# Two-layer hybrid decoder trunk: the first x piece travels with the norm's scale columns, the first AV weights come in halves, and two k tiles multiply their high parts first

## The chip, the cores and the metric

The kernel runs on one core of one Trainium2 chip. The metric is device time in microseconds (us), median of several runs; lower is better. Before the change it is 254.97 us (median of 3 runs, 254.91 to 255.15).

The names of the engines in this text: PE is TensorE (matmuls; PEld is its weight load), DVE is VectorE, ACT is ScalarE, POOL is GpSimd, SP is SyncE. SP computes nothing here, it issues DMAs. ACT issues a few as well.

## The reference, cut to what matters

A sequence of 256 tokens with 1024 channels passes two layers. Each layer normalizes x, projects it with one combined matrix `w_in` (1024 x 3584) into ten pieces, runs three mixers on them (dilated attention A, a gated linear recurrence B, stick-breaking attention C), gates each and projects back with `w_out`.

```python
def hybrid_layer(x, ...):
    hn = rms_norm(x, norm_gain)
    proj = jnp.einsum('bsd,de->bse', hn, w_in)
    a_q, a_k, a_v, a_g, b_x, b_g, c_q, c_k, c_v, c_g = jnp.split(proj, _in_split_points(), axis=-1)
    y_a = dilated_attention(rope(a_q), rope(a_k), a_v) * jax.nn.silu(a_g)
    y_b = rg_lru_branch(b_x, ...) * jax.nn.silu(b_g)
    y_c = stick_breaking_attention(c_q, c_k, c_v) * jax.nn.silu(c_g)
    y = jnp.concatenate([y_a, y_b, y_c], axis=-1)
    return x + jnp.einsum('bse,ed->bsd', y, w_out)
```

`rms_norm` divides each token by the root of its mean square and multiplies each channel by `norm_gain`. The kernel may therefore multiply x by the channel gains first, run the projections of layer 0 on that, and divide by the root per token afterwards.

## The kernel before

**Precision.** Every large product is done in three fp32r matmuls. An operand is split into a high part (a rounded copy) and a low part (the operand less its high part), and high x high, low x high and high x low are added up in one PSUM bank. So each 128-row piece of x becomes `xh` and `xl`, each piece of weights `hi` and `lo` (tiles `whi`, `wlo`). ACT makes the high parts by a copy, DVE the low parts by a subtraction.

**The opening stage**, which the change rewrites, is the loop over `k` (lines 133 to 155). It computes two projections of layer 0 that need x as the stationary operand: AV (512 columns, two PSUM banks `s`, one for each half of the tokens) and CV (256 columns, two banks `pp`). There are NK = 8 pieces `k` of 128 channels. One DMA brings for a piece its transposed x (256 columns) and its AV and CV weights (512 + 256 columns) as one 128 x 1024 tile `st`; the pool has 5 such tiles, so pieces 5 to 7 are issued when an older tile has been read. ACT multiplies x by the gain column `g` while it copies it to `xh`, then copies the weights to `hi`; DVE makes `xl` and `lo`. PE then runs six pairs of matmuls for the piece: AV high, AV low x, AV low weights, CV high, CV low x, CV low weights, each for two halves of the tokens.

Piece 0 is special. It is fetched by three DMAs, x (128 KB) and the CV weights (128 KB) on SP's queue, the AV weights (256 KB) on ACT's. ACT's queue also brings `prm_t`, a table of small parameters with the gain columns at its end; every `xh` needs it. Its AV weights are rounded by DVE (line 144) rather than ACT:

```python
        act.activation(xh[:, k, :], st[:, 0:S], AF.Copy, scale=g)
        if k == 0:
            dve.tensor_copy(hi[:, 0:512], st[:, S:S + 512])
            act.activation(hi[:, 512:768], st[:, S + 512:1024], AF.Copy)
```

Ahead of the loop PE runs seven matmuls on zeros (line 131), and ACT loads its function table.

**After it** the remaining projections go chunk by chunk through `proj_b` (line 262; 48 matmuls of 256 columns a chunk, in two halves), in the order CQ, CK, AQ, AK, BX and so on. Each chunk's weights arrive as two DMAs on SP's queue (line 100), ACT rounds them in four copies (line 103) and DVE subtracts in four (line 104). Between the halves of CK, `rows_of_rstd` turns the token scales into a row (lines 293 to 299). Then `scaled` writes the stick-breaking query `qc` and key `kc` (line 311), and `sb_scores` (line 353) multiplies them on PE inside the AQ projection. `rp0` (line 500) is the rotary table times the token scales, used by `rotate` for AQ and AK. `sb_weights` (line 380) later multiplies `sh` and `sl`, the split softplus of the scores.

**Order.** PE's order is the order in which the code is written. ACT, DVE, POOL and SP are ordered by the framework's scheduler, so their streams may shift when the code changes. `log_sigmoid_lambda` (line 219) is a chain of tiny operations on POOL, DVE and ACT that reads `prm_t`; its result is needed by the recurrence much later.

Of the kernel before, what the change touches and what calls it, by code (L numbers as in the profile page):

```python
# [38 lines left out]
SM_P = 16  # L39
# [5 lines left out]


@with_exitstack
def trunk_kernel(ctx: ExitStack, tc: tile.TileContext, x, first, wpack, prm_d, gatew, gains, consts, rope, out):
    nc = tc.nc
    act, dve, pe, gps = nc.scalar, nc.vector, nc.tensor, nc.gpsimd  # L50

    cst = ctx.enter_context(tc.tile_pool(name="cst", bufs=1))
    wst = ctx.enter_context(tc.tile_pool(name="wst", bufs=WST))
    wsp = ctx.enter_context(tc.tile_pool(name="wsp", bufs=4))
    sb = ctx.enter_context(tc.tile_pool(name="sb", bufs=1))
# [36 lines left out]
    xh = sb.tile([P, NK, S], F32R, name="xh", tag="xh")  # L92
    xl = sb.tile([P, NK, S], F32R, name="xl", tag="xl")

    def load_chunk(l, c):
        hi = wsp.tile([P, 2048], F32R, name="whi", tag="whi")
        lo = wsp.tile([P, 2048], F32R, name="wlo", tag="wlo")
        for i in range(2):
            st = wst.tile([P, 1024], F32, name="st", tag="st")
            nc.sync.dma_start(out=st, in_=wpack[l, c][:, i * 1024:(i + 1) * 1024])  # L100
            for j in range(0, 1024, 512):
                ws, ss = slice(i * 1024 + j, i * 1024 + j + 512), slice(j, j + 512)
                act.activation(hi[:, ws], st[:, ss], AF.Copy)  # L103
                dve.tensor_sub(lo[:, ws], st[:, ss], hi[:, ws].bitcast(F32))  # L104
        return hi, lo
# [11 lines left out]

    cold = sb.tile([P, 512], BF16, name="cold", tag="th")
    dve.memset(cold, 0.0)
    prm_t = cst.tile([P, L * SM_P + NK], F32, name="prm_t")  # L120
    st0 = [wst.tile([P, 1024], F32, name="st", tag="st")]
    nc.sync.dma_start(out=st0[0][:, 0:S], in_=first[0][:, 0:S])
    act.dma_start(out=st0[0][:, S:S + 512], in_=first[0][:, S:S + 512])
    act.dma_start(out=prm_t, in_=prm_d)
    nc.sync.dma_start(out=st0[0][:, S + 512:1024], in_=first[0][:, S + 512:1024])
    table(LN_EXP)
    av_ps = [bank(at, "s") for _ in range(NT)]
    cv_bk = [bank(pp, "pp") for _ in range(NT)]
# [2 lines left out]
        pe.matmul(warm, cold[:, 0:P], cold, start=True, stop=True)  # L131
    pair = None
    for k in range(NK):
        st = st0[0] if k == 0 else wst.tile([P, 1024], F32, name="st", tag="st")
        if k > 0:
            nc.sync.dma_start(out=st, in_=first[k])
        g = prm_t[:, L * SM_P + k:L * SM_P + k + 1]
        if k % 2 == 0:
            pair = [wsp.tile([P, 2048], F32R, name=n, tag=n) for n in ("whi", "wlo")]
        o = k % 2 * 768  # L140
        hi, lo = [a[:, o:o + 768] for a in pair]
        act.activation(xh[:, k, :], st[:, 0:S], AF.Copy, scale=g)
        if k == 0:
            dve.tensor_copy(hi[:, 0:512], st[:, S:S + 512])
            act.activation(hi[:, 512:768], st[:, S + 512:1024], AF.Copy)
        else:
            act.activation(hi, st[:, S:1024], AF.Copy)
        dve.scalar_tensor_tensor(xl[:, k, :], st[:, 0:S], g, xh[:, k, :].bitcast(F32), ALU.mult, ALU.subtract)
        for c in ((0, 512), (512, 768)) if k == 0 else ((0, 768),):
            dve.tensor_sub(lo[:, c[0]:c[1]], st[:, S + c[0]:S + c[1]], hi[:, c[0]:c[1]].bitcast(F32))  # L150
        for ps, c in ((av_ps, slice(0, 512)), (cv_bk, slice(512, 768))):
            for i, (a, b) in enumerate(((xh, hi), (xl, hi), (xh, lo))):
                for t in range(NT):
                    pe.matmul(ps[t][:, 0:c.stop - c.start], a[:, k, t * P:(t + 1) * P], b[:, c],  # L154
                              start=k == 0 and i == 0, stop=k == NK - 1 and i == 2)
# [61 lines left out]
    nc8 = cst.tile([P, L * 2], F32, name="nc8")  # L217

    def log_sigmoid_lambda():
        lam = prm_t[:, 0:L * SM_P].rearrange("p (q j) -> p q j", q=2 * L)[:, :, 7:8].rearrange("p b j -> p (b j)")  # L220
# [28 lines left out]
    for l in range(L):  # L249
        prm = prm_t[:, l * SM_P:(l + 1) * SM_P].rearrange("p (b j) -> p b j", b=2)  # L250
        if l > 0:
            xh, xl = next_x
# [23 lines left out]
        if l > 0:  # L276
# [3 lines left out]
            av_ps, cv_ps = [], bank(pp, "pp")  # L280
# [7 lines left out]
            cv_bk = [cv_ps[:, t * 256:(t + 1) * 256] for t in range(NT)]  # L288
# [19 lines left out]
        def scaled(dst, ps, sc=1.0):  # L308
            if l == 0:
                a, b = rows(ps)  # L310
                dve.scalar_tensor_tensor(dst, a, sc, b, ALU.mult, ALU.mult)  # L311
            else:
                act.activation(dst, v2(ps), AF.Copy, scale=sc)
# [5 lines left out]
        gw = gw_t.rearrange("p (g b c) -> p g b c", g=2, b=2)  # L319
# [30 lines left out]
        kc = sb.tile([P, 2, S], F32, name="kc", tag="k1")  # L350
# [91 lines left out]
        it = sb.tile([P, 2, S], F32, name="it", tag="it")  # L442
# [53 lines left out]
        ck_ps = proj_b(CH_CK, rows_of_rstd if l == 0 else None)  # L496
        if l == 0:
            scaled(qc, cq_ps, 0.125)
            for i in range(2):
                dve.tensor_mul(rp0[:, i, :], rp[:, i, :], rb)  # L500
        scaled(kc, ck_ps)
        rotate(proj_b(CH_AQ[0], sb_scores), qT, 0, "q0")
        rotate(proj_b(CH_AK[0], lambda: sb_weights(0)), kT, 0, "k0")
        sb_weights(1)
# [128 lines left out]
    return wp  # L633


def _pack_small(norm_gain, conv_w, conv_b, gate_a_w, gate_a_b, gate_x_w, gate_x_b, lru_lambda):
    pr = np.zeros((P, L * SM_P + NK), np.float32)
    pr[:, L * SM_P:] = norm_gain[0].reshape(NK, P).T
    gw = np.zeros((P, L, SM_W), np.float32)
    for l in range(L):  # L640
        for b in range(2):
            r = slice(b * P, b * P + P)
            o = l * SM_P + 8 * b
            pr[:, o:o + 4] = conv_w[l][:, r].T
            pr[:, o + 4] = conv_b[l][r]
            pr[:, o + 5] = gate_a_b[l].reshape(-1)[r]
            pr[:, o + 6] = gate_x_b[l].reshape(-1)[r]
            pr[:, o + 7] = lru_lambda[l][r]
            for g, w in enumerate((gate_a_w, gate_x_w)):
                c = (g * 2 + b) * P  # L650
                for j in range(2):
                    gw[j * HD:(j + 1) * HD, l, c + j * HD:c + (j + 1) * HD] = w[l, 2 * b + j]
    return pr, gw


def _arrays(x, norm_gain, w_in, conv_w, conv_b, gate_a_w, gate_a_b, gate_x_w, gate_x_b,
            lru_lambda, w_out, final_gain):
# [32 lines left out]
```

## Time and profile before

| | |
|---|---|
| median of 3 runs | 254.97 us |
| the profiled execution's own time | 255.37 us |
| its span, first to last instruction | 253.6 us |
| PE busy | 245.1 us (97%) |
| DVE busy | 190.3 us (75%) |
| ACT busy | 164.2 us (65%) |
| POOL busy | 12.9 us (5%) |
| chain of work that ended last | PE 95%, DMA 1%, ACT 1% |
| bytes moved | 43.44 MB |

The profile is one execution. A row of the timeline has the start of a group of instructions and its length in us, the engine, the line, the operation, its output and input tiles, the shapes, how many it merges, and in brackets how long the engine sat idle before it and what ended that. An engine name with a q behind it (SPq, ACTq) is the engine's queue issuing a DMA; the length is then that of the issue, not of the transfer. Matmuls overlap, so the distance between the starts of two groups tells what a group costs. All times in this document are us from the first instruction of the span unless they are lengths.

### The profile page before, as it was taken

What the parts mean: (1) busy time and instruction counts of PE and PEld (TensorE: products, weight loads), DVE (VectorE), ACT (ScalarE), POOL (GpSimd) and SP (SyncE); (2) the same over time, 40 slices, a digit from 0 to 9 for tenths busy, and PEclk for the clock granted to TensorE, in tenths of its full rate; (3) what the DMA queues carried; (4) which work ended last, traced back from release to release, by engine and by line L of the source; (5) the groups of instructions that cost most, each with busy time, mean ns of one, the idle gap of its engine ahead of it and who ended that gap; (6) DMA issues with size and microseconds to landing.
All of it is one profiled execution on the core that took longest, in us unless ns stands there. A gap on an engine that the chain in (4) does not pass through costs nothing.

```text
span 253.6 us, 4715 instructions
## 1 busy us (share of the span) xinstructions
PE 245.1 (97%) x1771; PEld 223.7 (88%) x1771; DVE 190.3 (75%) x424; ACT 164.2 (65%) x355; POOL 12.9 (5%) x35
## 2 busy tenths in 40 slices
PE   6999999999999999999999999999999999999990
PEld 2889999998999989878889999999899998987870
DVE  4684498999999669988692754399999846984243
ACT  3767958953675875994762865593495596794143
POOL 1186000000000000000010000000000000000000
PEclk9999999999999999999999999999999999999999
DMA  6989988844337840158457486531734732000022
GB/s 195 363 270 386 349 297 307 283 190 145 105 121 230 269 159 14 59 188 257 162 173 240 138 291 237 168 123 45 226 109 156 233 109 84 3 0 0 3 83 83
DMA packets 12982, 43.44 MB, mean 171 GB/s; under 512 B 1568, under 2 KB 1952, under 8 KB 12960
## 3 DMA queue, kind: packets, MB, share of 16 engines
q1 hardware_dynamic: 12672, 42.87, 49.6%
q8 instruction: 14, 0.23, 0.3%
q10 hardware_dynamic: 288, 0.28, 0.3%
q14 instruction: 8, 0.07, 0.1%
HBM read 42.09 MB, written 1.05 MB: 170 GB/s over the span
## 4 chain that ended last, share of the span: by engine, by line
PE 95%; DMA 1%; ACT 1%; DVE 0%; issue 0%; SPq 0%; ACTq 0%
PE pp L195 65%; PE s L195 9%; PE s L154 5%; PE y L345 3%; PE pp L154 2%; PE s L413 2%; PE s L435 2%; PE s L386 1%; PE pp L461 1%; DMA st<-first 1%; PE s L359 1%; PE s L211 1%; PE s L366 0%; PE s L384 0%; PE s L362 0%; ACT scr L177 0%
## 5 line engine op out<-in xcount | busy, mean ns | idle before, releaser
L104 DVE TENSOR_TENSOR wlo<-st,whi 128x512 fp32r<-128x512 f32 x132 | 84.9, 686 | 22.4 <-ACT whi L103 21.3
L103 ACT ACTIVATE whi<-st 128x512 fp32r<-128x512 f32 x132 | 74.5, 623 | 28.6 <-PE pp L195 10.4
L195 PE MATMUL pp<-xh,whi 128*128 128x256 f32 x352 | 50.3, 285 | 0.0
L195 PE MATMUL pp<-xl,whi 128*128 128x256 f32 x352 | 49.4, 283 | 0.0
L195 PE MATMUL pp<-xh,wlo 128*128 128x256 f32 x352 | 49.4, 283 | 0.0
L195 PEld LDWEIGHTS pp<-xh,whi 128*128 128x128 f32 x352 | 45.8, 191 | 1.4 <-issue 1.3
L195 PEld LDWEIGHTS pp<-xh,wlo 128*128 128x128 f32 x352 | 45.4, 192 | 0.0
L195 PEld LDWEIGHTS pp<-xl,whi 128*128 128x128 f32 x352 | 45.4, 192 | 0.0
L82 ACT ACTIVATE pr<-scr,mn 128x128 f32<-128x128 f32 (+1 forms) x32 | 14.1, 441 | 10.3 <-DVE mn L421 10.3
L177 ACT ACTIVATE scr<-xres 128x512 f32<-128x512 f32 x12 | 7.5, 626 | 12.5 <-DVE xres L569 12.4
L195 PE MATMUL pp<-whi,yh 128*128 128x512 f32 x48 | 14.1, 394 | 0.0
L195 PE MATMUL pp<-whi,yl 128*128 128x512 f32 x48 | 13.8, 390 | 0.0
L195 PE MATMUL pp<-wlo,yh 128*128 128x512 f32 x48 | 13.8, 390 | 0.0
L333 ACT ACTIVATE yh<-scr 128x512 fp32r<-128x512 f32 x8 | 5.0, 631 | 13.1 <-DVE scr L332 13.1
L179 POOL TENSOR_SCALAR ss<-sq 128x1 f32<-128x1 f32 x6 | 1.8, 306 | 221.0 <-ACT scr L177 220.9
L76 ACT ACT_TABLE_LOAD x9 | 11.5, 1283 | 1.8 <-PEq L683 1.6
L82 ACT ACTIVATE scr<-scr 128x384 f32<-128x384 f32 (+1 forms) x20 | 10.8, 542 | 1.2 <-DVE scr L311 0.9
L195 PEld LDWEIGHTS pp<-wlo,yh 128*128 128x128 f32 x48 | 9.0, 188 | 1.9
L195 PEld LDWEIGHTS pp<-whi,yl 128*128 128x128 f32 x48 | 9.0, 188 | 1.9
L421 DVE CUSTOM_DVE_ANT_0 scr<-s,con 128x128 f32<-128x128 f32 (+1 forms) x32 | 10.2, 347 | 0.0
L195 PEld LDWEIGHTS pp<-whi,yh 128*128 128x128 f32 x48 | 8.7, 188 | 1.6
L569 DVE TENSOR_TENSOR xres<-pp,xres 128x512 f32<-128x512 f32 x6 | 4.1, 690 | 6.7 <-PE pp L195 6.6
(158 smaller groups left out, 360.0 us busy)
## 6 DMA issues: line engine op xcount, KB each, us to landing
st<-w_pack SPq DMA_DIRECT2D x66, 512.0 KB, 4.8
st<-first SPq DMA_DIRECT2D x7, 512.0 KB, 6.9
xres<-x_in SPq DMA_DIRECT2D x2, 512.0 KB, 8.3
out<-scr SPq DMA_DIRECT2D x4, 256.0 KB, 2.2
gw_t<-gate_w SPq DMA_DIRECT2D x2, 256.0 KB, 6.7
gn<-gains SPq DMA_DIRECT2D x1, 512.0 KB, 6.5
gf<-gains SPq DMA_DIRECT2D x1, 512.0 KB, 5.6
st<-first ACTq DMA_DIRECT2D x1, 256.0 KB, 3.2
```

What stands on the lines that cost most here:

```text
L76: load = act.preload_act_table_set(name)
L82: i = dep(act.activation(*a, **k), loaded["load"])
L103: act.activation(hi[:, ws], st[:, ss], AF.Copy)
L104: dve.tensor_sub(lo[:, ws], st[:, ss], hi[:, ws].bitcast(F32))
L154: pe.matmul(ps[t][:, 0:c.stop - c.start], a[:, k, t * P:(t + 1) * P], b[:, c], start=k == 0 and i == 0, stop=k == NK - 1 and i == 2)
L177: act.activation(scr(512), xres[:, t, i * 512:(i + 1) * 512], AF.Square, accum_out=sq[:, i:i + 1])
L195: pe.matmul(ps, a(k), b(k), start=first and i == 0, stop=last and i == len(seq) - 1)
L333: act.activation(yh[:, k0:k0 + n, :], dst, AF.Copy)
L345: pe.matmul(y[hr, p * 128 + o:p * 128 + 256], vt[:, s0, hs], wts[i][:, ws], start=s0 == 0, stop=s0 == 1)
L413: pe.matmul(sps[h][:, cs], qT[h0][hr, hb, t * P:(t + 1) * P], kT[h0][hr, hb, 0:(t + 1) * P], start=True, stop=True)
L421: dve.tensor_tensor_reduce(xs[:, cs], sps[h][:, cs], nmask[:, cs], -0.125, 3e38, ALU.add, ALU.min, mn[:, t:t + 1])
L435: pe.transpose(tp[:, i * P:(i + 1) * P], prob[h0 + h][:, j * P:(j + 1) * P], ident)
```

## The change

It does four things.

1. The gain columns leave `prm_t` and are put behind the x piece of `k` = 0 in an array of their own, `first_x` (128 x 264). One DMA at the head of SP's queue brings both into a tile `x0`. All eight gain columns are then read from `x0`. `prm_t`, now without them, is fetched on SP's queue behind the eight pieces of the loop.
2. The 512 AV weight columns of piece 0 come as two DMAs of 256 columns, one on ACT's queue and one on SP's; the 256 CV columns move to ACT's queue. DVE rounds the two halves apart, and PE multiplies them apart for `k` = 0 (256 columns instead of 512, twice as many matmuls of half the size).
3. For `k` = 0 and 1 PE runs all high x high products (AV and CV) first, then all with low x, then all with low weights. For `k` = 1 too, DVE rounds the AV weights and ACT only the CV weights.
4. `kc` is written ahead of the two products for `rp0`.

```diff
-    prm_t = cst.tile([P, L * SM_P + NK], F32, name="prm_t")
-    st0 = [wst.tile([P, 1024], F32, name="st", tag="st")]
-    nc.sync.dma_start(out=st0[0][:, 0:S], in_=first[0][:, 0:S])
-    act.dma_start(out=st0[0][:, S:S + 512], in_=first[0][:, S:S + 512])
-    act.dma_start(out=prm_t, in_=prm_d)
-    nc.sync.dma_start(out=st0[0][:, S + 512:1024], in_=first[0][:, S + 512:1024])
+    x0 = sb.tile([P, S + NK], F32, name="x0", tag="it")
+    st0 = wst.tile([P, 1024], F32, name="st", tag="st")
+    nc.sync.dma_start(out=x0, in_=first_x)
+    act.dma_start(out=st0[:, S:S + 256], in_=first[0][:, S:S + 256])
+    nc.sync.dma_start(out=st0[:, S + 256:S + 512], in_=first[0][:, S + 256:S + 512])
+    act.dma_start(out=st0[:, S + 512:1024], in_=first[0][:, S + 512:1024])
...
-        g = prm_t[:, L * SM_P + k:L * SM_P + k + 1]
+        x_in = x0 if k == 0 else st
+        g = x0[:, S + k:S + k + 1]
...
-        act.activation(xh[:, k, :], st[:, 0:S], AF.Copy, scale=g)
-        if k == 0:
-            dve.tensor_copy(hi[:, 0:512], st[:, S:S + 512])
-            act.activation(hi[:, 512:768], st[:, S + 512:1024], AF.Copy)
+        w = st[:, S:1024]
+        act.activation(xh[:, k, :], x_in[:, 0:S], AF.Copy, scale=g)
+        for c0, c1 in {0: ((0, 256), (256, 512)), 1: ((0, 512),)}.get(k, ()):
+            dve.tensor_copy(hi[:, c0:c1], w[:, c0:c1])
+        if k < 2:
+            act.activation(hi[:, 512:768], w[:, 512:768], AF.Copy)
         else:
-            act.activation(hi, st[:, S:1024], AF.Copy)
+            act.activation(hi, w, AF.Copy)
...
+        parts = ((av_ps, 0, 0, 256), (av_ps, 0, 256, 512)) if k == 0 else ((av_ps, 0, 0, 512),)
+        parts += ((cv_bk, 512, 512, 768),)
+        terms = tuple(enumerate(((xh, hi), (xl, hi), (xh, lo))))
+        seq = [(i, p) for i in terms for p in parts] if k < 2 else [(i, p) for p in parts for i in terms]
+        for (i, (a, b)), (ps, base, c0, c1) in seq:
+            for t in range(NT):
+                pe.matmul(ps[t][:, c0 - base:c1 - base], a[:, k, t * P:(t + 1) * P], b[:, c0:c1],
...
+    prm_t = cst.tile([P, L * SM_P], F32, name="prm_t")
+    nc.sync.dma_start(out=prm_t, in_=prm_d)
     ready[pending.pop(0)] = load_chunk(0, CH_CQ)
...
             scaled(qc, cq_ps, 0.125)
+        scaled(kc, ck_ps)
+        if l == 0:
             for i in range(2):
                 dve.tensor_mul(rp0[:, i, :], rp[:, i, :], rb)
-        scaled(kc, ck_ps)
```

**PE, pieces 0 and 1.** In these rows `s` are the AV banks, `pp` the CV banks, and the two tiles behind the arrow are the two operands. Before:

```order
L154 MATMUL s<-whi,xh 128x512 x2
L154 MATMUL s<-whi,xl 128x512 x2
L154 MATMUL s<-wlo,xh 128x512 x2
L154 MATMUL pp<-whi,xh 128x256 x2
L154 MATMUL pp<-whi,xl 128x256 x2
L154 MATMUL pp<-wlo,xh 128x256 x2
L154 MATMUL s<-whi,xh 128x512 x2
```

With the change, the same engine at the same place:

```order
L160 MATMUL s<-whi,xh 128x256 x4
L160 MATMUL pp<-whi,xh 128x256 x2
L160 MATMUL s<-whi,xl 128x256 x4
L160 MATMUL pp<-whi,xl 128x256 x2
L160 MATMUL s<-wlo,xh 128x256 x4
L160 MATMUL pp<-wlo,xh 128x256 x2
L160 MATMUL s<-whi,xh 128x512 x2
L160 MATMUL pp<-whi,xh 128x256 x2
L160 MATMUL s<-whi,xl 128x512 x2
L160 MATMUL pp<-whi,xl 128x256 x2
```

The CV products with high parts have moved ahead of the AV products with low parts; from piece 2 on the order is as it was.

**ACT, its first instructions.** `st<-first` are weights of piece 0, `x_85` is the new tile `x0`. Before:

```order
L123 DMA st<-first 128x512
L124 DMA prm_t<-prm 128x40
L76 ACT_TABLE_LOAD
L145 ACTIVATE whi<-st 128x256
L142 ACTIVATE xh<-st,prm_t 128x256 x2
L147 ACTIVATE whi<-st 128x768
```

With the change:

```order
L123 DMA st<-first 128x256
L125 DMA st<-first 128x256
L76 ACT_TABLE_LOAD
L144 ACTIVATE xh<-x_85 128x256
L148 ACTIVATE whi<-st 128x256
L144 ACTIVATE xh<-st,x_85 128x256
L148 ACTIVATE whi<-st 128x256
L144 ACTIVATE xh<-st,x_85 128x256
L150 ACTIVATE whi<-st 128x768
```

The copy of the x piece now stands ahead of the CV weights, waits for `x0` alone, and the weight copy of piece 1 is a third as wide.

**DVE, around the stick-breaking scores.** Here `whi`, `wlo` are chunks of the later projections, `kc` the key, `rp_285` and `rp_296` the scaled rotary table, `sh` and `sl` the split softplus of the first head. Before:

```order
L311 SCALAR_TENSOR_TENSOR qc<-pp,rb 128x512
L104 TENSOR_TENSOR wlo<-st,whi 128x512 x4
L500 TENSOR_TENSOR rp_285<-rp,rb 128x256 x2
L311 SCALAR_TENSOR_TENSOR kc<-pp,rb 128x512
L104 TENSOR_TENSOR wlo<-st,whi 128x512 x8
L374 SCALAR_TENSOR_TENSOR scr<-s,scr 128x384
L377 CAST sh<-scr 128x384
L104 TENSOR_TENSOR wlo<-st,whi 128x512
L378 TENSOR_TENSOR sl<-scr,sh 128x384
```

With the change:

```order
L320 SCALAR_TENSOR_TENSOR qc<-pp,rb 128x512
L104 TENSOR_TENSOR wlo<-st,whi 128x512 x4
L320 SCALAR_TENSOR_TENSOR kc<-pp,rb 128x512
L511 TENSOR_TENSOR rp_296<-rp,rb 128x256 x2
L104 TENSOR_TENSOR wlo<-st,whi 128x512 x7
L383 SCALAR_TENSOR_TENSOR scr<-s,scr 128x384
L104 TENSOR_TENSOR wlo<-st,whi 128x512
L386 CAST sh<-scr 128x384
L104 TENSOR_TENSOR wlo<-st,whi 128x512
L387 TENSOR_TENSOR sl<-scr,sh 128x384
```

`kc` stands two instructions earlier. The scheduler has also moved one weight subtraction of the eight behind the softplus.

More of the change, by code (lines that the diff above doesn't have):

```diff
@@ L47, in trunk_kernel @@
 @with_exitstack
-def trunk_kernel(ctx: ExitStack, tc: tile.TileContext, x, first, wpack, prm_d, gatew, gains, consts, rope, out):
+def trunk_kernel(ctx: ExitStack, tc: tile.TileContext, x, first_x, first, wpack, prm_d, gatew, gains, consts, rope, out):
     nc = tc.nc
@@ L133, in trunk_kernel @@
     for k in range(NK):
-        st = st0[0] if k == 0 else wst.tile([P, 1024], F32, name="st", tag="st")
+        st = st0 if k == 0 else wst.tile([P, 1024], F32, name="st", tag="st")
         if k > 0:
             nc.sync.dma_start(out=st, in_=first[k])
-        g = prm_t[:, L * SM_P + k:L * SM_P + k + 1]
+        x_in = x0 if k == 0 else st
+        g = x0[:, S + k:S + k + 1]
         if k % 2 == 0:
@@ L141, in trunk_kernel @@
         hi, lo = [a[:, o:o + 768] for a in pair]
-        act.activation(xh[:, k, :], st[:, 0:S], AF.Copy, scale=g)
-        if k == 0:
-            dve.tensor_copy(hi[:, 0:512], st[:, S:S + 512])
-            act.activation(hi[:, 512:768], st[:, S + 512:1024], AF.Copy)
-        else:
[L147 to L155, printed above, removed]
+        w = st[:, S:1024]
+        act.activation(xh[:, k, :], x_in[:, 0:S], AF.Copy, scale=g)
+        for c0, c1 in {0: ((0, 256), (256, 512)), 1: ((0, 512),)}.get(k, ()):
+            dve.tensor_copy(hi[:, c0:c1], w[:, c0:c1])
@@ new lines, in trunk_kernel @@
+        if k < 2:
+            act.activation(hi[:, 512:768], w[:, 512:768], AF.Copy)
+        else:
+            act.activation(hi, w, AF.Copy)
+        dve.scalar_tensor_tensor(xl[:, k, :], x_in[:, 0:S], g, xh[:, k, :].bitcast(F32), ALU.mult, ALU.subtract)
+        for c0, c1 in ((0, 512), (512, 768)) if k < 2 else ((0, 768),):
+            dve.tensor_sub(lo[:, c0:c1], w[:, c0:c1], hi[:, c0:c1].bitcast(F32))
+        parts = ((av_ps, 0, 0, 256), (av_ps, 0, 256, 512)) if k == 0 else ((av_ps, 0, 0, 512),)
@@ new lines, in trunk_kernel @@
+        parts += ((cv_bk, 512, 512, 768),)
[4 more added lines that the diff above has]
+                pe.matmul(ps[t][:, c0 - base:c1 - base], a[:, k, t * P:(t + 1) * P], b[:, c0:c1],
+                          start=k == 0 and i == 0 and c0 == base, stop=k == NK - 1 and i == 2,
+                          skip_group_check=True)
@@ L219, in log_sigmoid_lambda @@
     def log_sigmoid_lambda():
-        lam = prm_t[:, 0:L * SM_P].rearrange("p (q j) -> p q j", q=2 * L)[:, :, 7:8].rearrange("p b j -> p (b j)")
+        lam = prm_t.rearrange("p (q j) -> p q j", q=2 * L)[:, :, 7:8].rearrange("p b j -> p (b j)")
         def tn(name):
@@ L633, in _pack_weights, with _pack_small @@
     return wp
-def _pack_small(norm_gain, conv_w, conv_b, gate_a_w, gate_a_b, gate_x_w, gate_x_b, lru_lambda):
-    pr = np.zeros((P, L * SM_P + NK), np.float32)
-    pr[:, L * SM_P:] = norm_gain[0].reshape(NK, P).T
+def _pack_small(conv_w, conv_b, gate_a_w, gate_a_b, gate_x_w, gate_x_b, lru_lambda):
+    pr = np.zeros((P, L * SM_P), np.float32)
     gw = np.zeros((P, L, SM_W), np.float32)
@@ L661, in _arrays @@
     x2 = x.reshape(S, D)
-    pr, gw = _pack_small(norm_gain, conv_w, conv_b, gate_a_w, gate_a_b, gate_x_w, gate_x_b, lru_lambda)
+    pr, gw = _pack_small(conv_w, conv_b, gate_a_w, gate_a_b, gate_x_w, gate_x_b, lru_lambda)
     return {
         "x_in": np.ascontiguousarray(x2),
+        "first_x": np.concatenate([x2.T[0:P], norm_gain[0].reshape(NK, P).T], 1),
         "first": np.concatenate([x2.T.reshape(NK, P, S), w_in[0].reshape(NK, P, 3584)[:, :, 1024:1536],
```

## The prediction

> **What bounds the kernel now.** I read the page first, then PE's waits, then the timeline of the opening.
>
> ```profile
> span 253.6 us, 4715 instructions
> ...
> PE 245.1 (97%) x1771; PEld 223.7 (88%) x1771; DVE 190.3 (75%) x424; ACT 164.2 (65%) x355; POOL 12.9 (5%) x35
> ```
>
> PE works nearly all the span. The view of its waits lists one besides that for its very first operand:
>
> ```profile
> PE s L154 <- ACT xh L142: 0.9, 1, 0.9
> ```
>
> From its first real matmul on, PE never waits. The change leaves PE's products the same, so it can gain only in the opening: by what it saves there, less what a later wait gives back. The timeline of the opening:
>
> ```profile
> 0.71 0.41 ACTq L123 DMA_DIRECT2D st<-first  x1
> 0.72 0.37 SPq L122 DMA_DIRECT2D st<-first  x1
> ...
> 1.15 0.42 SPq L125 DMA_DIRECT2D st<-first  x1
> 1.16 0.45 ACTq L124 DMA_DIRECT2D prm_t<-prm  x1
> ...
> 1.17 3.17 PE L131 MATMUL y<-cold 128*128 128x512 bf16 x7 [1.17 <-DVE cold L119]
> ...
> 1.61 10.27 SPq L136 DMA_DIRECT2D st<-first  x7
> ...
> 3.96 0.43 DVE L144 CAST whi<-st 128x512 fp32r<-128x512 f32 x1 [2.43 <-DMA st<-first]
> 4.34 0.42 ACT L145 ACTIVATE whi<-st 128x256 fp32r<-128x256 f32 x1 [1.42 <-DMA st<-first]
> 4.42 0.69 DVE L150 TENSOR_TENSOR wlo<-st,whi 128x512 fp32r<-128x512 f32 x1
> ...
> 4.66 0.49 ACT L142 ACTIVATE xh<-st,prm_t 128x256 fp32r<-128x256 f32 x1
> 5.19 0.48 DVE L148 SCALAR_TENSOR_TENSOR xl<-st,prm_t,xh 128x256 fp32r<-128x256 f32 x1
> ...
> 5.21 1.22 PE L154 MATMUL s<-whi,xh 128*128 128x512 f32 x2 [0.87 <-ACT xh L142]
> ...
> 6.23 1.05 PE L154 MATMUL s<-whi,xl 128*128 128x512 f32 x2
> ...
> 7.08 1.05 PE L154 MATMUL s<-wlo,xh 128*128 128x512 f32 x2
> ...
> 7.96 0.51 ACT L142 ACTIVATE xh<-st,prm_t 128x256 fp32r<-128x256 f32 x1 [2.81 <-DMA st<-first]
> ...
> 8.38 0.83 ACT L147 ACTIVATE whi<-st 128x768 fp32r<-128x768 f32 x1
> ...
> 9.26 1.09 PE L154 MATMUL s<-whi,xh 128*128 128x512 f32 x2
> 9.65 0.83 ACT L147 ACTIVATE whi<-st 128x768 fp32r<-128x768 f32 x1
> ...
> 10.18 0.62 PE L154 MATMUL s<-whi,xl 128*128 128x512 f32 x2
> ...
> 11.09 0.40 PE L154 MATMUL pp<-whi,xh 128*128 128x256 f32 x2
> ...
> 11.80 0.63 PE L154 MATMUL s<-whi,xh 128*128 128x512 f32 x2
> ```
>
> Three things are to be seen. Piece 0 starts at 5.21, piece 1 at 9.26, piece 2 at 11.80. Piece 1 was on time by a hair: its weight copy ran 8.38 to 9.21. And PE changes speed: a pair of 512-column matmuls takes 0.85 early (6.23 to 7.08) and 0.46 later (two pairs from 10.18 to 11.09). The pair at 9.26 took 0.92, so the full clock came at about 10.0, inside it. Three pairs of 256 columns then take 11.80 - 11.09 = 0.71, so 0.24 each, half of the 0.46. (The profile's granted-clock row reads full here too; the spacing says otherwise.)
>
> **Piece 0.** From issue to landing the transfers issued in the first 2 us took (the list of DMA issues for that window; the 512 KB one is piece 1):
>
> ```profile
> st<-first SPq DMA_DIRECT2D x1, 512.0 KB, 6.3
> st<-first SPq DMA_DIRECT2D x2, 128.0 KB, 3.1
> prm_t<-prm ACTq DMA_DIRECT2D x1, 20.0 KB, 3.3
> ```
>
> Before, `xh` was ready only after `prm_t` (1.16 + 3.3 = 4.46) and after the CV copy ahead of it on ACT. Now it waits for `x0` alone: at the median of its kind 0.72 + 3.1 = 3.8. From the start of `xh` to PE's first matmul were 5.21 - 4.66 = 0.55, so PE starts at about 4.35, as the seven matmuls on zeros end (1.17 + 3.17 = 4.34). The first weight half is a 128 KB transfer issued at 0.71; its cast of half of 0.43 is done by 4.1. The second half is issued second on SP: 1.15 + 3.1 = 4.25, cast by 4.5, needed after two matmuls at 0.21, at 4.8. The CV weights land at 4.3 and are copied in 0.42; PE wants them at 5.2. `xl` (0.48) is done by 5.0, wanted at 5.6. So piece 0 runs without a hole, and the idle 0.87 goes. The six extra weight loads I cost at nothing, because matmuls of 256 columns take half of those of 512 (0.24 and 0.46 a pair), so their loads are hidden already; uncovered they could cost one such matmul each, 6 x 0.21 = 1.3, in a piece that has 1.3 to spare, as will be seen.
>
> **The clock.** How long piece 0 lasts depends on when the full clock comes. Before, PE was busy 1.17 to 4.34, idle 0.87, and got it about 4.8 after the restart. With no hole, PE will have been busy from 1.17 on. If the count starts there, the clock comes at about 1.17 + 4.8 = 6.0; that it stays at 10.0 is case (a) below. I take 6.0. Piece 0 has 18 matmuls of 256 columns: (6.0 - 4.35) / 0.213 = 7.7 of them slow, 10.3 at 0.118, the end at 7.2. Anything up to 8.5 would do as well, as the next part shows.
>
> [...]
>
> **Piece 1** is then what PE waits for. Its 512 KB transfer is still third on SP, issued at 1.61, 6.3 to landing: 7.9. SP issues two DMAs ahead of it as before, and the bytes ahead of it fall by the 20 KB of `prm_t` only, so I leave it there. ACT's `xh` starts at 7.96 and PE can start at 7.96 + 0.55 = 8.51, for the AV weights are now cast by DVE beside it (0.43), not copied behind it. High products: AV 0.46, CV 0.23 (its copy, 0.42, is done at 8.80), to 9.20. DVE does the cast (0.43), the AV low weights (0.69) and then `xl` (0.48); with the pitches of the rows before (4.42 - 3.96 = 0.46, then about 0.61) `xl` ends at 9.51 and PE goes on at 9.56, after 0.36 of waiting. Low x 0.69, low weights 0.69: piece 1 ends at 10.94. Before, it ended at 11.80. **The gain is 0.86.** Piece 2 is there: its copies cannot be later than before, 9.65 + 0.83 = 10.48. From then on PE runs as before, 0.86 earlier.
>
> **What comes next.** Being earlier only counts if the later data are there. The tightest places behind, with PE's start of each:
>
> ```profile
> 27.87 4.58 ACT L103 ACTIVATE whi<-st 128x512 fp32r<-128x512 f32 x8
> ...
> 30.16 1.12 PE L195 MATMUL pp<-xh,whi 128*128 128x256 f32 x8
> ...
> 37.49 0.76 DVE L500 TENSOR_TENSOR rp<-rp,rb 128x256 f32<-128x256 f32 x2
> 38.16 0.69 DVE L311 SCALAR_TENSOR_TENSOR kc<-pp,rb 128x512 f32<-128x512 f32 x1
> ...
> 39.33 0.70 PE L359 MATMUL s<-qc,kc 64*128 64x256 f32 x4
> ...
> 46.21 0.55 DVE L378 TENSOR_TENSOR sl<-scr,sh 128x384 fp32r<-128x384 f32 x1
> ...
> 47.40 0.22 PE L384 MATMUL s<-sl,trir 128*128 128x128 f32 x1
> ```
>
> Chunk CK: the fourth of eight weight copies ends at about 27.87 + 4 x 0.57 = 30.15, and PE wants it at its seventh matmul, 30.16 + 6 x 0.12 = 30.88. The spare of 0.73 is less than 0.86. The loads behind these copies are issued when earlier pieces have been read, which DVE does somewhat sooner now, so the cost lies between 0 and 0.13; I take 0.06. `kc` ended at 38.85 with 0.48 to spare; it now stands ahead of two products that took 38.16 - 37.49 = 0.67, which gives 1.15. (`rp0`, so much later, is first read after the AQ projection.) `sl` ended at 46.76 with 0.64 to spare. It follows from three steps of ACT on the scores, and the scheduler has put one weight copy fewer (0.57) ahead of them, so about 1.2. Without either move PE would wait 0.86 - 0.48 = 0.38 at `kc` and 0.22 at `sl`.
>
> `prm_t` moves behind eight pieces of 512 KB. POOL's first step waits for it, DVE's next, and behind that on DVE stand the low weights of piece 7, on ACT the copies of CQ:
>
> ```profile
> 17.48 0.96 DVE L150 TENSOR_TENSOR wlo<-st,whi 128x768 fp32r<-128x768 f32 x1 [0.25 <-ACT whi L147]
> ...
> 19.23 1.16 ACT L103 ACTIVATE whi<-st 128x512 fp32r<-128x512 f32 x2 [1.79 <-DMA st<-w_pack]
> ```
>
> PE needs piece 7's low weights at about 11.80 + 5 x 2.1 + 1 = 23.3 before, 22.4 now, so 4 us cover it, and ACT had idled 1.79 there. I cost it at nothing; uncovered it would be the 3.3 of a small transfer.
>
> **The sum.** 0.86 - 0.06 = 0.80. The profiled execution took 255.37, span 253.6 and 1.77 around it; it becomes 254.57. It stood 0.40 above the median, so against the median I predict 254.97 - 0.80 = 254.17.
>
> **Rivals.** (a) The clock does not come sooner: it stays at 10.0. Then piece 0 ends at 4.35 + 3.84 = 8.2, piece 1 starts at 8.51 at half speed: high products to 9.79, low x to 10.6, low weights to 11.3. The gain is 0.5, the time 254.5. For it: the trace shows one opening only, and the matmuls on zeros may not count. Against: the clock stayed at half for nine us from 1.17, and the hole is the only interruption in them.
>
> (b) No gain: piece 1 lands later, or a later wait returns it. The page's list of issues gives all seven 512 KB pieces a median that is 0.6 above piece 1's 6.3:
>
> ```profile
> st<-first SPq DMA_DIRECT2D x7, 512.0 KB, 6.9
> ```
>
> If piece 1 lands 0.6 later because the queues are filled in another order, the gain is 0.2, at 0.8 none: 254.8 to 255.0. The row of piece 1 itself speaks against it, since what is ahead of it changes by 20 KB.
>
> (c) Slower, by the clock. PE now waits 1.3 (7.2 to 8.5) for piece 1 just after the full clock came, where before there was no hole from then on. If that takes the clock back, PE has to work another 4.8 for it; at half speed that loses 2.4, less the 0.80 won: 1.6 slower, 256.6. It decides at the hole's length: below what takes the clock, nothing. The end of the kernel speaks against it:
>
> ```profile
> 245.60:249.00 3.40, 1.55 (x7) 0.94 (x5) 1.81 (x3) 1.31 (x5) 0.19 (x1) 1.00 0.32 119
> 249.00:252.40 3.40, 0.00 (x0) 0.00 (x0) 0.56 (x2) 0.95 (x3) 0.00 (x0) 1.00 0.42 154
> 252.40:253.60 1.20, 0.00 (x0) 0.00 (x0) 0.00 (x0) 0.00 (x0) 0.00 (x0) 0.50 0.00 0
> ```
>
> The first number behind the length is PE's busy time, and the third from the end is the granted clock. PE's last work ended at 245.60 + 1.55 = 247.15, and the clock fell at 252.40, after 5.2 of idle time, four times the hole. [...]
>
> **How the numbers follow.** Chances: my case 0.66, (a) 0.17, (b) 0.12, (c) 0.05. A difference of 0.2% (0.5 us) is about what a measurement of this kernel can tell. Faster by more: nearly all of my case and a third of (a), which lies on the bound: 0.70. Within: the rest of (a), nearly all of (b), some of mine: 0.24. Slower: (c) and a little: 0.06. The range: below, piece 2's copies end at 10.48, so piece 1 cannot usefully end before that; the gain is at most 1.3, 253.65, and the scatter of the runs, 254.91 to 255.15, makes it 253.5. Above it takes in (a) and half of (b): 254.8.
>
> **What would show it.** PE's wait for `xh` at 5.21 gone and piece 0 at about 4.35; a pair of 512 columns at 0.46 from piece 1's first product on; a PE wait of about 1.3 for piece 1 and one of 0.3 to 0.4 for its `xl`; piece 2 at about 10.9; no wait over 0.15 at CK, `kc` or `sl`. Half speed in piece 1 would mean (a), a full-speed opening with PE waits further on (b), half speed again after piece 1 (c).

## The result and the profile after

The changed kernel takes 257.62 us in the median (257.42 to 258.27, 6 runs), the kernel before 254.94 beside it (253.57 to 255.53, 6 runs). The ratio is 1.0116, with a 95% interval of 1.009 to 1.0142. It is slower by 2.7 us where 0.8 faster was forecast, and far above the forecast's range of 253.5 to 254.8. The profiled execution of after took 257.5. Its page, the span, the busy time and the chain that ended last:

```profile
span 255.7 us, 4729 instructions
...
PE 246.3 (96%) x1777; PEld 225.1 (88%) x1777; DVE 190.8 (75%) x427; ACT 164.3 (64%) x355; POOL 9.6 (4%) x35
...
PE 86%; DMA 4%; ACT 3%; POOL 3%; issue 1%; DVE 1%; SPq 0%; ACTq 0%
```

The span has grown by 2.1 us, and the chain, which before lay on PE for 95%, now passes through POOL. An engine that is busy for 4% of the span has come to decide something.

**The opening went better than forecast.** The timeline of after, pieces 0 to 2:

```profile
3.64 0.51 ACT L144 ACTIVATE xh<-x 128x256 fp32r<-128x256 f32 x1 [0.73 <-DMA x<-first_x]
...
4.25 1.20 PE L160 MATMUL s<-whi,xh 128*128 128x256 f32 x4
...
5.78 0.51 ACT L144 ACTIVATE xh<-st,x 128x256 fp32r<-128x256 f32 x1 [0.82 <-DMA st<-first]
...
6.53 0.63 PE L160 MATMUL pp<-whi,xl 128*128 128x256 f32 x2
...
6.95 0.73 PE L160 MATMUL s<-wlo,xh 128*128 128x256 f32 x4
...
7.51 0.40 PE L160 MATMUL pp<-wlo,xh 128*128 128x256 f32 x2
...
7.75 0.63 PE L160 MATMUL s<-whi,xh 128*128 128x512 f32 x2
...
9.85 0.40 PE L160 MATMUL s<-whi,xh 128*128 128x512 f32 x1
```

Piece 0 starts at 4.25 without a wait (5.21 before), piece 1 at 7.75 (9.26), piece 2 at 9.85 (11.80). The full clock comes at about 7.1: a pair of 256 columns takes 0.42 at 6.53 and 0.24 at 7.51. PE is 1.95 ahead in this execution.

**Then it loses 4.** PE's waits in after have one new line (in all, times, longest):

```profile
PE pp L204 <- ACT whi L103: 1.7, 1, 1.7
```

The timeline of PE from chunk CQ to the scale products in the middle of CK, before (whose row for the start of CK stands in the prediction). Where this text gives a length for CK, it is that of its first half, up to these products.

```profile
24.40 1.12 PE L195 MATMUL pp<-xh,whi 128*128 128x256 f32 x8
...
33.05 0.60 PE L298 MATMUL y<-scr,ones 128*128 128x128 f32 x4
```

and after:

```profile
22.43 1.12 PE L204 MATMUL pp<-xh,whi 128*128 128x256 f32 x8
...
30.09 2.35 PE L204 MATMUL pp<-xh,whi 128*128 128x256 f32 x8 [1.73 <-ACT whi L103]
32.24 1.91 PE L204 MATMUL pp<-xl,whi 128*128 128x256 f32 x8
33.95 1.34 PE L204 MATMUL pp<-xh,wlo 128*128 128x256 f32 x8
35.13 0.60 PE L307 MATMUL y<-scr,ones 128*128 128x128 f32 x4
```

The stretch lasted 33.05 - 24.40 = 8.65 and now lasts 35.13 - 22.43 = 12.70. Of the loss of 4.05, the hole ahead of CK is 1.90 (CQ takes 30.16 - 24.40 = 5.76, so it ends at 28.19), and CK itself is longer by 2.15 (5.04 for 2.89). Less the 1.97 gained at CQ, this is the span's 2.1. The windows of after (first figure: length; second: PE's busy time; third from the end: the granted clock) show why CK itself is longer:

```profile
27.63:31.04 3.41, 1.66 (x11) 1.11 (x9) 0.97 (x2) 3.38 (x10) 0.00 (x0) 1.00 0.63 245
31.04:34.45 3.41, 3.39 (x16) 3.31 (x16) 3.41 (x9) 3.41 (x8) 0.00 (x0) 0.50 0.47 163
34.45:37.87 3.42, 3.42 (x31) 3.42 (x31) 3.25 (x7) 1.42 (x3) 0.00 (x0) 1.00 0.87 260
```

After a stretch in which PE worked 1.66 of 3.41, the clock fell to half for exactly the next 3.41.

**Who was late.** CK's weights wait for ACT, ACT for POOL, POOL for the table. POOL's timeline before:

```profile
4.55 0.64 POOL L226 TENSOR_SCALAR ls<-prm_t 128x4 f32<-128x4 f32 x1 [3.74 <-DMA prm_t<-prm]
...
22.89 0.51 POOL L242 TENSOR_SCALAR nc<-c 128x4 f32<-128x4 f32 x1
23.48 0.19 POOL L179 TENSOR_SCALAR ss<-sq 128x1 f32<-128x1 f32 x1
```

and after:

```profile
15.08 0.63 POOL L235 TENSOR_SCALAR ls<-prm_t 128x4 f32<-128x4 f32 x1 [14.26 <-DMA prm_t<-prm]
...
25.08 0.22 POOL L251 TENSOR_SCALAR nc<-c 128x4 f32<-128x4 f32 x1
25.38 0.19 POOL L188 TENSOR_SCALAR ss<-sq 128x1 f32<-128x1 f32 x1
```

ACT's timeline, before:

```profile
23.18 0.19 ACT L177 ACTIVATION_READ_ACCUMULATOR scr<-xres 128x1 f32 x1
...
24.07 0.29 ACT L82 ACTIVATE lnv<-sq,ss 128x1 f32<-128x1 f32 x1
```

and after:

```profile
22.31 0.19 ACT L186 ACTIVATION_READ_ACCUMULATOR scr<-xres 128x1 f32 x1
...
25.61 0.29 ACT L82 ACTIVATE lnv<-sq,ss 128x1 f32<-128x1 f32 x1 [2.49 <-POOL ss L188]
...
29.05 0.47 ACT L315 ACTIVATE vc<-pp,rstd 128x256 f32<-128x256 f32 x1
29.41 5.31 ACT L103 ACTIVATE whi<-st 128x512 fp32r<-128x512 f32 x10
```

`ls`, `c` and `nc` are the chain of `log_sigmoid_lambda`, some 24 small steps on POOL. `ss` is a part of the mean square of a token tile (`rms_stats`), which has nothing to do with the table; it only stands behind the chain in POOL's queue. Its input was there at 22.50 (22.31 + 0.19) and it ran at 25.38. ACT stood 2.49 at `lnv`, with the second tile's squares, the copies `va` and `vc` out of PSUM and then the copies of CK behind it. Before, the chain ended at 23.40, and ACT did not wait.

### The profile page after: what moved, and what is told of

Read it like the earlier page. It is cut to its first block, busy times and chain, and to the rows that moved or that the text cites. A ratio compares the mean times of both kernels' runs of the same rounds, so it can differ in the third digit from the quotient of the medians.

```text
span 255.7 us, 4729 instructions
## 1 busy us (share of the span) xinstructions
PE 246.3 (96%) x1777; PEld 225.1 (88%) x1777; DVE 190.8 (75%) x427; ACT 164.3 (64%) x355; POOL 9.6 (4%) x35
## 4 chain that ended last, share of the span: by engine, by line
PE 86%; DMA 4%; ACT 3%; POOL 3%; issue 1%; DVE 1%; SPq 0%; ACTq 0%
PE pp L204 64%; PE s L204 9%; DMA st<-first 4%; PE y L354 3%; PE s L422 2%; PE s L444 2%; PE s L395 1%; PE pp L470 1%; POOL ls L246 1%; POOL ls L245 1%; PE s L368 1%; PE s L220 1%; ACT scr L186 1%; ACT whi L150 1%; PE s L375 0%
## 5 line engine op out<-in xcount | busy, mean ns | idle before, releaser
L204 PE MATMUL pp<-xh,whi 128*128 128x256 f32 x352 | 51.5, 288 | 1.8 <-ACT whi L103 1.7
L204 PE MATMUL pp<-xl,whi 128*128 128x256 f32 x352 | 50.2, 286 | 0.0
L204 PEld LDWEIGHTS pp<-xl,whi 128*128 128x128 f32 x352 | 46.2, 195 | 0.0
```

The source lines that it names most:

```text
L204: pe.matmul(ps, a(k), b(k), start=first and i == 0, stop=last and i == len(seq) - 1)
```

## The experiments

Theory A: the table, moved behind eight pieces, makes POOL's chain late; `ss`, ACT and the copies of CK follow; PE's hole there and the clock that falls behind it cost the loss. Theory B: the loss comes from elsewhere in the change, the transfers' order or the order of products. Ratios are against the kernel before on the same chip, spans of the profiled executions stand last. Beside e1 to e4 before took 255.03, beside e5 to e8 255.08, beside e9 to e11 255.29.

| kernel | median (range, runs) | ratio, 95% interval | span |
|---|---|---|---|
| after | 257.62 (257.42-258.27, 6) | 1.0116, 1.009-1.0142 | 255.7 |
| e1_prm_early | 253.61 (253.31-255.27, 7) | 0.9935, 0.9921-0.9948 | 253.5 |
| e2_ss_on_dve | 253.28 (252.9-253.89, 6) | 0.9929, 0.9915-0.9943 | 252.1 |
| e3_prm_later_still | 254.11 (253.07-255.3, 12) | 0.9967, 0.9948-0.9986 | 251.4 |
| e4_filler | 256.52 (255.58-256.68, 6) | 1.0049, 1.0033-1.0064 | 254.7 |
| e5_before_prm_late | 258.04 (256.45-258.75, 6) | 1.0108, 1.0076-1.014 | 254.8 |
| e6_old_order | 254.81 (253.37-255.3, 12) | 0.9976, 0.9957-0.9995 | 252.2 |
| e7_kc_behind | 253.62 (252.91-254.75, 12) | 0.9954, 0.9933-0.9976 | 252.2 |
| e8_one_av_piece | 253.95 (252.71-254.89, 12) | 0.9966, 0.9944-0.9989 | 251.6 |
| e9_warm8 | 253.33 (252.84-254.56, 12) | 0.994, 0.9917-0.9962 | 251.6 |
| e10_ck_ahead | 254.71 (254.01-255.78, 12) | 0.9993, 0.9971-1.0014 | 253.0 |
| e11_ck_ahead_warm8 | 254.34 (253.45-255.49, 12) | 0.9981, 0.9958-1.0005 | 253.4 |

### e1_prm_early: the table early again

The changed kernel, with the table fetched third on ACT's queue.

```diff
     act.dma_start(out=st0[:, S + 512:1024], in_=first[0][:, S + 512:1024])
+    prm_t = cst.tile([P, L * SM_P], F32, name="prm_t")
+    act.dma_start(out=prm_t, in_=prm_d)
...
-    prm_t = cst.tile([P, L * SM_P], F32, name="prm_t")
-    nc.sync.dma_start(out=prm_t, in_=prm_d)
```

> The change, with the parameter table fetched third on ACT's queue in the opening, as before. Theory A (the late table starts POOL's lambda chain 10 us later, the mean-square step ss of the norm stands behind that chain on POOL, and through it ACT's evictions and the CK weight copies come late, PE waits 1.7 and the clock falls for 3.4): ss at about 22.5 instead of 25.4, CK copies from about 27.2 instead of 29.4, PE's wait at CK at most 0.4, no stretch at half clock, 253.2 to 253.7 us. Theory B (the CK copies are late because of the transfers, POOL's order does not matter): nothing changes, about 257.6.

Measured: the loss turns into a gain, ratio 0.9935. Its timeline of POOL:

```profile
22.19 0.19 POOL L188 TENSOR_SCALAR ss<-sq 128x1 f32<-128x1 f32 x1
```

and of ACT:

```profile
26.22 2.26 ACT L103 ACTIVATE whi<-st 128x512 fp32r<-128x512 f32 x4
```

The copies of CK start 3.2 earlier than in after, and PE does not wait there (in this trace it comes to CK only at 30.02, where after came at 28.19). The opening and the order of products stayed, so that half of theory B falls; the table's own transfer has moved, and e2 tells about that. This profiled execution was its slowest, 255.27, and its opening ran at half clock up to 9.83 at least, as the 0.85 for a pair of 512 columns shows:

```profile
8.98 1.05 PE L162 MATMUL s<-whi,xh 128*128 128x512 f32 x2
9.83 0.59 PE L162 MATMUL pp<-whi,xh 128*128 128x256 f32 x2
```

### e2_ss_on_dve: ss leaves POOL's queue

The changed kernel with the late table, and one word edited.

```diff
-        gps.tensor_scalar(ss, sq[:, 0:1], 1.0 / D, EPS, ALU.mult, ALU.add)
+        dve.tensor_scalar(ss, sq[:, 0:1], 1.0 / D, EPS, ALU.mult, ALU.add)
```

> The change with its late table, but the mean-square step ss is done by DVE instead of POOL, so that it no longer queues behind the lambda chain. Theory A: as with the early table, 253.2 to 253.7, although the table still lands at 15.0 and the lambda chain still ends at about 25.3. Theory B: about 257.6.

Measured: ratio 0.9929. The table is as late as in after, and the chain on POOL too. Every transfer stayed, so the other half of theory B falls as well. POOL's timeline:

```profile
14.97 0.30 POOL L235 TENSOR_SCALAR ls<-prm_t 128x4 f32<-128x4 f32 x1 [14.15 <-DMA prm_t<-prm]
...
24.85 0.22 POOL L251 TENSOR_SCALAR nc<-c 128x4 f32<-128x4 f32 x1
```

ACT's, with the copies of CK:

```profile
26.53 4.60 ACT L103 ACTIVATE whi<-st 128x512 fp32r<-128x512 f32 x8
```

and PE's:

```profile
27.84 1.44 PE L204 MATMUL pp<-xh,whi 128*128 128x256 f32 x8
29.11 1.12 PE L204 MATMUL pp<-xl,whi 128*128 128x256 f32 x8
30.07 1.12 PE L204 MATMUL pp<-xh,wlo 128*128 128x256 f32 x8
```

So it is not the late chain that costs, but what stands behind it in its queue. CK's first group takes 29.11 - 27.84 = 1.27 and the next one 0.96, so 0.3 is still lost.

### e3_prm_later_still: the table even later

The table's transfer goes behind the rope table and the gate weights; the framework's scheduler then puts `ss` ahead of the chain on POOL by itself.

```diff
-    nc.sync.dma_start(out=prm_t, in_=prm_d)
...
         nc.sync.dma_start(out=gw_t, in_=gatew[:, l, :])
+        if l == 0:
+            nc.sync.dma_start(out=prm_t, in_=prm_d)
```

> The change, with the table fetched later still, behind the rotary table and the gate weights; the scheduler then puts ss ahead of the lambda chain on POOL. If lateness of the table as such is the cause, this must be slower than 257.6. Theory A (only the place of ss behind the chain matters): ss at about 23, 253.2 to 253.9. Theory B: about 257.6.

POOL's timeline:

```profile
21.79 0.19 POOL L187 TENSOR_SCALAR ss<-sq 128x1 f32<-128x1 f32 x1 [20.97 <-ACT scr L185]
...
24.48 0.23 POOL L234 TENSOR_SCALAR ls<-prm_t 128x4 f32<-128x4 f32 x1 [0.89 <-DMA prm_t<-prm]
```

The table lands 9.4 later than in after, and the kernel is faster than before (0.9967). That a later table costs less follows from theory A: the place in the queue decides, not the arrival. (The median of 254.11 is 0.2 above what theory A expected.)

### e4_filler: the hole kept, the clock kept up

The changed kernel with seven matmuls on zeros between CQ and CK. They add work whose result nobody reads.

```diff
         if l == 0:
+            fill = bank(yp, "y")
+            for i in range(7):
+                pe.matmul(fill, cold[:, 0:P], cold, start=True, stop=True)
```

> The change, with seven idle matmuls on zeros on PE between CQ and CK, which fill about 1.5 of the 1.7 us hole and lead to no result. The CK copies stay late. If the hole is what takes the clock down at 31.0 (theory A's second half): no half-speed stretch, CK then bound by the copies and low parts, 1.2 to 1.6 us faster than the change, 256.0 to 256.4. If the clock falls for another reason, the same as the change or up to 0.2 slower, 257.6 to 257.8.

PE's timeline:

```profile
28.03 1.69 PE L499 MATMUL y<-cold 128*128 128x512 bf16 x7
30.18 2.06 PE L204 MATMUL pp<-xh,whi 128*128 128x256 f32 x8 [0.47 <-ACT whi L103]
...
34.00 0.60 PE L307 MATMUL y<-scr,ones 128*128 128x128 f32 x4
```

The same windows as of after:

```profile
27.63:31.04 3.41, 2.93 (x16) 1.55 (x14) 0.88 (x2) 3.38 (x9) 0.00 (x0) 1.00 0.55 219
31.04:34.45 3.41, 3.38 (x27) 3.01 (x26) 3.41 (x9) 3.41 (x8) 0.00 (x0) 1.00 0.49 151
```

CK starts as late as in after, but the clock stays full. CK then takes 34.00 - 30.18 = 3.82, which is 0.93 over the 2.89 of before (its first group takes 1.90 for 0.96; that PE is fed at the pace of ACT's copies there fits, but is not shown apart) and 1.22 less than the 5.04 of after. The clock's fall is worth 1.2 in the traces, and 1.0116 - 1.0049 = 0.67% or 1.7 in the ratios (two series of runs). The rest is the late data. The median of 256.52 is 0.1 above what was expected of a clock that holds. The mean granted clock that is on record for every run (the fall at the kernel's end is in it, too) says the same: 0.987 to 0.989 in all six runs of after, 0.991 to 0.997 in the six of e4 and 0.991 to 0.998 in those of before beside it.

### e5_before_prm_late: the late table alone

The kernel before, with nothing of the change but the late table.

```diff
-    prm_t = cst.tile([P, L * SM_P + NK], F32, name="prm_t")
-    act.dma_start(out=prm_t, in_=prm_d)
+    gain_t = cst.tile([P, NK], F32, name="gain_t")
+    act.dma_start(out=gain_t, in_=prm_d[:, L * SM_P:])
...
-        g = prm_t[:, L * SM_P + k:L * SM_P + k + 1]
+        g = gain_t[:, k:k + 1]
...
+    prm_t = cst.tile([P, L * SM_P], F32, name="prm_t")
+    nc.sync.dma_start(out=prm_t, in_=prm_d[:, 0:L * SM_P])
```

> The kernel before with one part of the change alone: the scale columns in a tile of their own, taken by ACT's queue where the table stood, and the table prm_t fetched by SP behind the eight x pieces. Opening order, x pieces and AV weights stay as before. Theory A (the late table holds POOL's gate chain, and ss stands behind it): the table lands at about 16.5, POOL's chain ends at about 26.5 instead of 23.4, ss follows it, ACT's copies of the CK operand end about 3 later than before, and PE waits about 1 there, since it reaches CK 2 later than in the changed kernel; 256.0 to 257.0, and up to 258 if the clock falls behind that wait. Theory B (the loss came from the opening's transfers or from the order of products, not from the table): the table may come late at no cost, 254.5 to 255.4.

It is slower by as much as the whole change, ratio 1.0108. Here too `ss` runs right behind the chain and the copies of CK come late:

```profile
25.46 0.19 POOL L181 TENSOR_SCALAR ss<-sq 128x1 f32<-128x1 f32 x1
```

```profile
29.48 5.31 ACT L103 ACTIVATE whi<-st 128x512 fp32r<-128x512 f32 x10
```

PE's timeline in its profiled execution, which with 256.57 was one of the two fastest of six:

```profile
30.16 2.06 PE L197 MATMUL pp<-xh,whi 128*128 128x256 f32 x8 [0.41 <-ACT whi L103]
...
33.98 0.60 PE L300 MATMUL y<-scr,ones 128*128 128x128 f32 x4
```

Here the hole is small (0.41) and the clock holds (1.00 in the three windows shown of after, 27.63 to 37.87); CK takes 3.82 as in e4. The other four runs, at 257.87 to 258.75, are 1.3 to 2.2 above it. There is no trace of them, but their mean granted clocks are on record: 0.989, 0.989 and 0.990 in the three slowest, below every run of before beside them (0.991 to 0.998), which speaks for a fall in those. The fourth, 257.87, has 0.996, and why it is slower stays open.

### e6, e7, e8: the other parts, each undone in e2

e6_old_order has the old order of products in the first two pieces:

```diff
-        seq = [(i, p) for i in terms for p in parts] if k < 2 else [(i, p) for p in parts for i in terms]
+        seq = [(i, p) for p in parts for i in terms]
```

> e2 (the changed kernel with ss on DVE) with the order of products of the kernel before in the first two k tiles, part by part, and the AV weights still in halves. If the new order carries a part of the opening's gain, PE waits for the second operands (the low halves) inside piece 0, 0.2 to 0.6 in all, and the time is 0.2 to 0.6 above e2 (253.5 to 253.9). Rival: the start of the first piece carries all of the gain and the order none, within 0.2 of e2 (253.1 to 253.5).

e7_kc_behind has `kc` back behind `rp0`:

```diff
-        scaled(kc, ck_ps)
         if l == 0:
             for i in range(2):
                 dve.tensor_mul(rp0[:, i, :], rp[:, i, :], rb)
+        scaled(kc, ck_ps)
```

> e2 with the scaled copy kc back behind the two rp0 products. If the forward place of kc is needed, a wait for kc of 0.4 to 0.9 shows ahead of the sb scores and the time is 0.3 to 0.8 above e2 (253.6 to 254.1). Rival: kc has room there (the forecast read a spare of 1.15 for it), no wait, within 0.2 of e2.

e8_one_av_piece has the AV weights of piece 0 in one transfer, one cast and 512-column products:

```diff
-    act.dma_start(out=st0[:, S:S + 256], in_=first[0][:, S:S + 256])
-    nc.sync.dma_start(out=st0[:, S + 256:S + 512], in_=first[0][:, S + 256:S + 512])
-    act.dma_start(out=st0[:, S + 512:1024], in_=first[0][:, S + 512:1024])
+    act.dma_start(out=st0[:, S:S + 512], in_=first[0][:, S:S + 512])
+    nc.sync.dma_start(out=st0[:, S + 512:1024], in_=first[0][:, S + 512:1024])
```

> e2 with the first AV weights in one piece of 256 KB again: one transfer, one cast, one subtraction, 512 wide products. If the halves matter, PE waits longer ahead of the first AV product (0.3 to 0.8 beside 0.5 in e2) and every later step of the opening moves by as much: 253.6 to 254.1. Rival: the halves only split one wait in two, within 0.2 of e2 (253.1 to 253.5).

PE's wait behind the opening's first in e6:

```profile
PE s L160 <- DVE xl L151: 0.8, 2, 0.5
```

in e7:

```profile
PE s L368 <- DVE kc L320: 0.2, 1, 0.2
```

and in e8:

```profile
PE s L159 <- DVE whi L145: 0.6, 1, 0.6
```

With the old order PE waits 0.8 in the first two pieces, and the median of e6 stands 0.9 to 1.2 above e7 and e8 of the same chip, more than expected. How much of that is the order is not shown: the twelve runs of e6 lie in two groups (253.4 to 254.0 and 254.8 to 255.3), and its profiled execution, of the faster one, has a span only 0.1 longer than e2's. `kc` ahead saves a wait of 0.2, against 0.4 to 0.9 expected. The halves shorten a wait by 0.1 (0.6 beside 0.5 in e2). The medians of e7 and e8 lie 0.3 and 0.7 above e2, but on another chip; the interval of e7's ratio overlaps that of e2, and e8's begins where that of e2 ends, so a small worth of the halves is neither shown nor ruled out.

### e9, e10, e11: towards a better version

e9 is e2 with eight warming products (`WARM = 8` for 7). e10 is e2 with the rope table and the gate weights fetched behind the weights of CK. e11 has both.

```diff
-        if l == 0:
-            nc.sync.dma_start(out=rp, in_=rope)
...
-        nc.sync.dma_start(out=gw_t, in_=gatew[:, l, :])
+        if l > 0:
+            nc.sync.dma_start(out=gw_t, in_=gatew[:, l, :])
...
         cq_ps = proj_b(CH_CQ)
+        if l == 0:
+            nc.sync.dma_start(out=rp, in_=rope)
+            nc.sync.dma_start(out=gw_t, in_=gatew[:, l, :])
```

> e2 with eight warming products in place of seven, so that PE is busy up to about 4.8 where e2 waited 0.5 (from 4.34 to 4.84) for the first AV weights. If that hole sometimes costs a window of the clock, the full clock opens in more of the runs by 6 to 7, and the median falls 0.1 to 0.5 below e2 (252.8 to 253.2) with less scatter. Rival: the hole decides nothing, or the eighth product delays the first AV product where the weights come earlier: within 0.2 of e2 or up to 0.2 above it (253.1 to 253.5).

> e2 with SP's transfers of the rope table and the gate weights moved behind the CK weights. In e2 the CK pieces land at 26.14 and 27.41 and PE's first CK group takes 1.44 where a group at its full pace takes 1.12. If these landings bind PE there, the CK pieces land some 1.3 earlier, the group takes 1.12 and the time falls 0.3 to 0.9 below e2 (252.4 to 253.0). Rival: ACT's evictions of va and vc hold the copies until 26.5 whatever has landed: no change against e2 (253.1 to 253.5), or slower if the rope table comes too late for its first use at 36.7.

> Both of the edits of the two runs beside this one, the eighth warming product and the CK weights ahead of the rope table: if each gives what is expected of it, they add up, 252.0 to 252.8; if neither does, 253.1 to 253.5 as e2.

e9 is e2 again (253.33, 0.994): its rival was right. e10 is a miss, 1.4 above e9 on the same chip. With CK's weights fetched earlier the scheduler put more of their subtractions ahead of the token scales on DVE, and PE waited for those; e11 has the same line with 0.8, and at 254.34 it is a miss of both its expectations. PE's waits in e10:

```profile
PE y L307 <- DVE scr L306: 0.9, 1, 0.9
```

It is the same kind of miss as the table's: a transfer that moves rearranges a queue that the expectation left out. e1, e2 and e9 stand lowest, 0.6 to 0.7% below before; e2 is the changed kernel with `ss` on DVE and nothing else.

## Why the prediction was wrong

**Piece 0** was right in after: 4.35 forecast, 4.25 measured, the idle 0.87 gone, and no hole in the piece. It is not so in every execution: in the traces of e1 and e2, with the same opening, PE waits 0.4 and 0.5 for the first AV weights.

**Piece 1 and the clock** were right in kind, wrong in size. "I leave it there" put the landing of piece 1 at 7.9; it landed at 5.75, and PE waited neither the 1.3 nor the 0.36 of the forecast. The single row of before was taken for a constant of this transfer. In e5, with the old opening, the `xh` that waits for it started at 6.62 (7.96 before). Why it differs stays open. The clock came at 7.1, not 6.0, which cost little. The gain was 1.95 for 0.86.

Some of that is luck. The forecast let the clock follow a count from PE's first work at 1.17; it follows no such count. By the spacing of the matmuls full speed came 6.0 behind that in after (at about 7.15), and 9.1 behind it in e1 (at about 10.26, from where a pair of 512 columns takes 0.47), whose trace is what rival (a) described: a clock that comes no sooner. There piece 2 starts at 11.66, a gain of 0.14 over before, where (a) had 0.5. In e2 piece 2 starts at 9.48. Without the wait at CK the change gains 1.7 (e1) to 1.8 (e2) us by the ratios, more than the 0.80 forecast.

**The step that failed is the table's:** "`prm_t` moves behind eight pieces of 512 KB. POOL's first step waits for it, DVE's next, and behind that on DVE stand the low weights of piece 7, on ACT the copies of CQ"; "I cost it at nothing". The queues of DVE and ACT were followed, POOL's own was not. There `ss` stood behind the chain, with no room at all: in the rows of before above, its input came at 23.37 (23.18 + 0.19) and POOL's chain ended at 23.40. The chain now starts at 15.08, ends at 25.30, and everything behind it is 2.9 late. This step costs 4.05 in the trace where nothing was put down, and e2 gets all but 0.3 of it back with one instruction. Rival (b) had "a later wait returns it", but named none and went no further than a gain of none.

**CK's spare** of 0.73 was read from copies that start at 27.87. With copies that start at 26.53 PE could come 2.3 earlier than before (27.84 for 30.16) and lose 0.3 (e2); with copies that start at 29.41 it could not.

**Rival (c)** had a hole that takes the clock back, at another place, and was given 0.05 because of the end of the kernel, where the clock held for 5.2 of idle time. That bound was wrong: a hole of 1.9 ahead of CK was enough. The stretch of 3.41 that it fell into was filled to 1.66, and with the hole filled the clock held (e4). At the end of before the clock was still full in a stretch without any PE work (249.00 to 252.40). How much PE work it takes to hold the clock these runs do not settle: it held behind a stretch of 3.41 with 2.93 of PE work (e4, at its hole) and fell behind the 1.66 of after, but it held behind 3.40 with 1.55 at the end of before (245.60 to 249.00), so PE's busy time alone does not decide.

## What to carry to other kernels

When a small transfer is moved back, follow every instruction that waits for it, and on each of those engines what stands behind it in the queue, unrelated work above all: the price is the spare of that, not of the data. An engine that is 4% busy can hold the chain, so look at its rows near the end of its chain, too, not only at its first step. And after a wait has been found, look at the granted clock of the next stretch: here it added nearly half as much again (1.2 to the 2.8 of late data).

## What was not expected of the hardware

The clock at the opening differs between runs of nearly the same work: it came at 7.1 in after, at about 10 in before and not ahead of 9.8 in e1. Whether short holes have a part in this the traces do not settle. After had none ahead of piece 0; before had one of 0.87. In e1 one of 0.43 (up to 4.77) went with half speed up to about 10.26; in e2 one of 0.50 at the same place (up to 4.84) did not, for from 5.90 four matmuls of 256 columns took 0.47, which is full speed. Before's 29 runs beside e5 to e8 span 253.38 to 255.59, where the first three lay within 0.24. A transfer of 512 KB, issued at the same 1.61, landed between 5.75 (after) and 7.94 (before), so a wait read from one trace of an opening is not good to better than that.
